# VectorE instructions on neighbouring 512-wide blocks merged, and PSUM tiles of two banks, in a two-layer encoder

## The chip, the core and the metric

The kernel runs on one core of a Trainium2 chip. TensorE (PE in the profile; PEld are its weight loads) multiplies into PSUM, VectorE (DVE) and ScalarE (ACT) work element by element, GpSimd (POOL) does small jobs, SyncE (SP) issues most of the DMAs. PSUM has eight banks, each one 128x512 fp32 result wide. The metric is the device time of one execution in microseconds (us); less is better.

## What is computed

A trunk of two layers over 256 tokens of width 2048, batch 1, in fp32:

```python
for l in range(DEPTH):
    h = rms_norm(x, g_mix[l])
    z = h @ (w_in_a[ia] if l % 2 == 0 else w_in_b[ib])
    tok_out = chunked_spatial_gating(...) if l % 2 == 0 else gqa_axial_attention(...)
    mem_out = memory_attention(q_mem, mem, g_mem[l], w_mem_kv[l], g_mq[l], g_mk[l])
    x = x + jnp.concatenate([tok_out, mem_out], axis=-1) @ w_out[l]
    x = x + swiglu(rms_norm(x, g_ffn[l]), w_gate_up[l], w_down[l])

def swiglu(h, w_gate_up, w_down):
    gate, up = jnp.split(h @ w_gate_up, 2, axis=-1)
    return (jax.nn.silu(gate) * up) @ w_down
```

The FFN is 5632 wide. Every weight is read once.

## The kernel before

**Precision.** Each operand of a product is split into a high part (a cast to fp32r, ScalarE, L192 and L254) and a low part (operand minus high part, VectorE, L193 and L255). `matmul3` (L196) then makes three matmuls: high by high, low by high, high by low. Weights are the moving operand, 512 columns wide; activations, transposed in 128x128 pieces on TensorE (L204), are the stationary one.

**Weights.** A weight tile `raw` holds four 128x512 blocks and comes by DMAs on SyncE's queue; four such tiles exist. `halves` (L248) makes its `whi` and `wlo` tiles, of which there are three each. In the mixers, `Linear.run` (L271) calls it with a step of two blocks, so that a unit of four blocks takes two casts and two subtractions; then come 24 matmuls, two blocks by two token tiles at a time. `Linear` has one accumulator bank for each of the two token tiles, out of the four of the pool `psa`.

**The FFN.** A `Pair` (L310) computes two neighbouring 512-column results for both token tiles: four results, from weight blocks w00, w10 (first column block, two rows of blocks) and w01, w11 (second). Its units are of two kinds. `eight` (L381) is the plain one: eight block products into banks 2 and 3 (token tile 0) and 4 and 8 (token tile 1). `seven` (L367) is a fast scheme with seven block products, on sums of weights and sums of activations: products 1, 5, 6 and 7 go to "inner" banks out of the pool `psm`, products 2, 3 and 4 into the outer banks. `prepare` (L339) fetches a unit's weights and, for a fast one, makes the four weight sums with four 512-wide additions (L347 to L350): t1 and t2, t3, t4 in `raw[:, 0]` and the tile `T`. It runs one unit ahead. After a Pair's last fast unit `inner` (L393) combines the four inner banks into e, f, v, y with one ScalarE copy and four VectorE instructions; for the down projection they are added into the residual x some steps later (L405). When the Pair's last unit is done `outer` (L408) adds banks 2 and 3, then 4 and 8, to the results (L413), one bank at a time.

A gate/up Pair's results go through SiLU (L785, L786) and are transposed some steps later by `turn_a` (L764), which takes a `misc` tile (L81), splits it and lets it go. `misc` tiles are single banks from `psm`, which has four; the mixers' transposes, attention scores and so on use them too. The FFN's eleven Pairs run in chunks of 4, 4 and 3, and after each chunk two Pairs of the down projection add into x.

**Order.** `later` and `tick` (L96, L99) place side work so many steps (half units) behind the point where it is queued. The program order that results is then reordered per engine by a planner that simulates the program and lets ready instructions go ahead of waiting ones; on the chip each engine runs its list in order. Tile pools are rings: a tile waits until the readers of the one before it in its place are done.

Of the kernel before, what the change touches and what calls it, by code (L numbers as in the profile page):

```python
# [10 lines left out]
F32 = mybir.dt.float32  # L11
# [5 lines left out]
P = 128  # L17
# [10 lines left out]
NB = 512  # L28
# [25 lines left out]
def encoder(ctx: ExitStack, tc: tile.TileContext, x, mem, g_mix, g_ffn, w_in_a, g_v_a, w_spatial, b_spatial,  # L54
# [10 lines left out]
    psa = ctx.enter_context(tc.tile_pool(name="psa", bufs=4, space=PS))  # L65
    psm = ctx.enter_context(tc.tile_pool(name="psm", bufs=4, space=PS))
# [13 lines left out]

    def misc():  # L81
        return psm.tile([P, NB], F32, tag="m", name=nm("m"))
# [37 lines left out]
    X = [[xp.tile([P, NB], F32, name=f"x_{t}_{j}") for j in range(4)] for t in range(NT)]  # L120
# [10 lines left out]
    def gain_columns(kind):  # L131
        gcol[kind] = const.tile([P, 32], F32, name=f"gcol_{kind}")
        gps = misc()
        nc.tensor.transpose(gps[:, :32], gst[kind], ident[:32, :32])
        nc.vector.tensor_copy(gcol[kind], gps[:, :32])
# [112 lines left out]
    def halves(raw, n, step=KC4):  # L248
# [3 lines left out]
        for c in range(0, n, step):  # L252
            cut = slice(c, min(c + step, n))
            nc.scalar.copy(hi[:, cut], raw[:, cut])  # L254
            nc.vector.tensor_tensor(lo[:, cut], raw[:, cut], hi[:, cut].bitcast(F32), ALU.subtract)  # L255
        return [(hi[:, c, :], lo[:, c, :]) for c in range(n)]

    class Linear:


        def __init__(self, parts, w, n0, nk=KD):
            self.parts, self.w, self.n0, self.left, self.first, self.raw = parts, w, n0, nk, True, {}
            self.acc = [psa.tile([P, NB], F32, tag="acc", name=nm("acc")) for _ in range(NT)]
# [7 lines left out]
        def run(self, units):  # L271
            for k0, n in units:
# [3 lines left out]
                parts = halves(raw[:, :n], n, KC2)  # L276
# [33 lines left out]
    class Pair:  # L310
# [5 lines left out]
        def __init__(self, parts, sums, w, na, nb, order, fast, into=None):  # L316
            self.parts, self.sums, self.w, self.na, self.nb, self.into = parts, sums, w, na, nb, into
            self.bank, self.part, self.ready = {}, {}, {}
# [20 lines left out]
        def prepare(self, i):  # L339
# [5 lines left out]
            if i in self.fast:  # L345
                T = room["p"].tile([P, KC3, NB], F32, tag="T", name=nm("T"), bufs=2)
                nc.vector.tensor_tensor(raw[:, 0], raw[:, 0], raw[:, 1], ALU.add)  # L347
                nc.vector.tensor_tensor(T[:, 0], raw[:, 0], raw[:, 3], ALU.add)
                nc.vector.tensor_tensor(T[:, 1], T[:, 0], raw[:, 1], ALU.subtract)
                nc.vector.tensor_tensor(T[:, 2], T[:, 0], raw[:, 2], ALU.add)  # L350
# [9 lines left out]
        def add(self, name, a, b):  # L360
            if name not in self.bank:
                self.bank[name] = misc() if name in (1, 5, 6, 7) else psa.tile([P, NB], F32, tag="acc", name=nm("acc"))
                self.part[name] = 0
# [3 lines left out]
        def seven(self, i, raw, T):  # L367
            t1, w00, w10, w11 = halves(raw, KC4)
            t2, t3, t4 = halves(T, KC3)
            get, (q5, s2, q7, q3) = self.parts.get, self.sums[i]  # L370
            k0, k1 = 2 * i, 2 * i + 1
            inner = [(1, get(k0, 0), w00), (5, q5, t1), (6, s2, t2), (7, q7, t3)]
            outer = [(2, get(k1, 0), w10), (3, q3, w11), (4, get(k1, 1), t4)]
            if self.bank:
                inner, outer = inner[:1] + outer[:2], inner[1:] + outer[2:]
# [17 lines left out]
        def inner(self):  # L393

            b, o = self.bank, self.into
            e, v, f, y = [room["p"].tile([P, NB], F32, tag=f"e{i}", name=nm("e"), bufs=1) for i in range(4)]
            nc.scalar.copy(e, b[1])
            nc.vector.tensor_tensor(v, b[6], e, ALU.subtract)
            nc.vector.tensor_tensor(f, b[5], v, ALU.add)
            nc.vector.tensor_tensor(v, b[7], v, ALU.add)  # L400
            nc.vector.tensor_tensor(y, b[7], f, ALU.add)
            if o:
                for (t, n), x, op in (((0, 0), e, ALU.add), ((0, 1), f, ALU.add), ((1, 0), v, ALU.subtract),
                                      ((1, 1), y, ALU.add)):
                    later(1 + 2 * t + n, lambda o=o[t][n], x=x, op=op: nc.vector.tensor_tensor(o, o, x, op))  # L405
            self.out = o or [[e, f], [v, y]]

        def outer(self, t):  # L408

            o = self.out  # L410
            for n, name in enumerate(((2, 3), (4, 8))[t]):
                op = ALU.subtract if name == 4 and not self.into else ALU.add
# [435 lines left out]
```

## Time and profile before

| | |
|---|---|
| runs before | median 2039.67 us of 3, 2039.08 to 2039.71 |
| profiled execution | span 2038.5 us, from first to last instruction (the page gives no other time of it) |
| HBM read | 390.26 MB, 194 GB/s over the span |
| weight casts L254 (ScalarE), on `raw` | 465 instructions, 700.8 us |
| weight subtractions L255 (VectorE), on `raw` | 465 instructions, 836.4 us |
| matmuls | 9298, most of them 128x512 |

A row of the groups reads: line, engine, operation, written tile <- read tiles, shape, count | busy us in all, mean ns of one | us that the engine sat idle just before them, and what ended most of that. A row of the timeline reads: start us, length us, engine, line, operation; in square brackets the engine's idle time ahead of it. A row of the stretches gives the stretch's borders and length, then each engine's busy us and instruction count, the clock granted to TensorE, the share of DMA time and GB/s.

### The profile page before, as it was taken

The numbers are of one execution on the slowest core, as the hardware profiler recorded it, in microseconds if no ns is written. First come the engines' busy times: TensorE is split into PE (matmuls) and PEld (weight loads), VectorE is DVE, ScalarE is ACT, GpSimd is POOL, SyncE is SP. The second block draws the span as 40 slices with busy tenths as digits, with TensorE's granted clock in tenths as the row PEclk, the third lists the DMA queues.
The fourth block names the chain that finished last, engine by engine and source line by source line (L and its number), as shares of the span: only waits on it lengthen the run. The fifth ranks groups of instructions, "written<-read, shape, count | busy, mean of one in ns | idle before, by whom it ended". The sixth has DMA issues, their size and how long they took to land.

```text
span 2038.5 us, 24693 instructions
## 1 busy us (share of the span) xinstructions
PE 2027.7 (99%) x9298; PEld 1679.9 (82%) x9298; DVE 1605.0 (79%) x1862; ACT 1095.0 (54%) x1389; POOL 50.6 (2%) x80
## 2 busy tenths in 40 slices
PE   9999999999999999999999999999999999999999
PEld 7888888888888888888888888888888888888887
DVE  5675557998879988887566886589979899798876
ACT  7765455454445554444555765555544455444552
POOL 2010000000000000000010100000000000000000
PEclk9999999999999999999999999999999999999999
DMA  9754554646656465665566544555566555565554
GB/s 325 253 179 155 185 188 154 227 165 206 203 190 227 165 207 196 202 227 194 186 198 204 173 133 141 202 185 178 195 206 218 195 184 190 205 221 192 183 197 137
DMA packets 202432, 396.08 MB, mean 194 GB/s; under 512 B 11068, under 2 KB 11432, under 8 KB 202312
## 3 DMA queue, kind: packets, MB, share of 16 engines
q1 hardware_dynamic: 198800, 385.79, 56.6%
q0 software_dynamic: 2048, 6.42, 1.0%
q10 hardware_dynamic: 1464, 2.28, 0.3%
q8 instruction: 73, 1.20, 0.2%
q14 instruction: 47, 0.39, 0.1%
HBM read 390.26 MB, written 4.19 MB: 194 GB/s over the span
## 4 chain that ended last, share of the span: by engine, by line
PE 96%; DVE 3%; DMA 1%; issue 1%; ACT 0%; SPq 0%; DVEq 0%; ACTq 0%
PE acc L200 27%; PE acc L199 27%; PE acc L198 27%; PE m L200 4%; PE m L198 4%; PE m L199 4%; PE m L204 2%; DVE wlo L255 1%; DMA raw<-in_w_gate_up 1%; PE m L500 0%; PE m L643 0%; ACT whi L254 0%; DVE x L413 0%; DVE e L413 0%; DMA x<-in_x 0%
## 5 line engine op out<-in xcount | busy, mean ns | idle before, releaser
L254 ACT CAST whi<-raw 128x2048 fp32r<-128x2048 f32 (+2 forms) x465 | 700.8, 1539 | 585.0 <-PE acc L199 512.5
L255 DVE TENSOR_TENSOR wlo<-raw,whi 128x2048 fp32r<-128x2048 f32 (+2 forms) x465 | 836.4, 1823 | 223.9 <-ACT whi L254 220.1
L198 PE MATMUL acc<-whi,h 128*128 128x512 f32 x1440 | 563.7, 392 | 0.0
L199 PE MATMUL acc<-whi,h 128*128 128x512 f32 x1440 | 562.6, 391 | 0.0
L200 PE MATMUL acc<-wlo,h 128*128 128x512 f32 x1440 | 524.1, 392 | 0.9 <-DVE wlo L255 0.9
L198 PE MATMUL acc<-whi,a 128*128 128x512 f32 x1062 | 414.8, 391 | 0.0
L199 PE MATMUL acc<-whi,a 128*128 128x512 f32 x1062 | 414.2, 390 | 0.0
L200 PE MATMUL acc<-wlo,a 128*128 128x512 f32 x1062 | 398.2, 391 | 0.0
L200 PEld LDWEIGHTS acc<-wlo,h 128*128 128x128 f32 x1440 | 270.6, 188 | 56.6 <-DVE wlo L255 1.5
L199 PEld LDWEIGHTS acc<-whi,h 128*128 128x128 f32 x1440 | 270.7, 188 | 55.3
L198 PEld LDWEIGHTS acc<-whi,h 128*128 128x128 f32 x1440 | 271.0, 188 | 54.0
L200 PEld LDWEIGHTS acc<-wlo,a 128*128 128x128 f32 x1062 | 199.4, 188 | 41.3 <-DVE wlo L255 0.3
L199 PEld LDWEIGHTS acc<-whi,a 128*128 128x128 f32 x1062 | 199.5, 188 | 40.4
L198 PEld LDWEIGHTS acc<-whi,a 128*128 128x128 f32 x1062 | 199.5, 188 | 40.2
L254 ACT CAST whi<-T 128x1536 fp32r<-128x1536 f32 x82 | 121.4, 1480 | 143.8 <-PE acc L199 102.2
L255 DVE TENSOR_TENSOR wlo<-T,whi 128x1536 fp32r<-128x1536 f32 x82 | 143.5, 1750 | 39.1 <-ACT whi L254 39.0
L198 PE MATMUL m<-whi,a 128*128 128x512 f32 x264 | 104.2, 395 | 0.7 <-ACT whi L254 0.7
L199 PE MATMUL m<-whi,a 128*128 128x512 f32 x264 | 102.9, 390 | 0.0
L347 DVE TENSOR_TENSOR raw<-raw 128x512 f32<-128x512 f32 x82 | 56.1, 684 | 54.9 <-DMA raw<-in_w_gate_up 53.5
L200 PE MATMUL m<-wlo,a 128*128 128x512 f32 x264 | 89.6, 389 | 0.0
L192 ACT CAST a<-m 128x512 fp32r<-128x512 f32 x80 | 46.7, 587 | 42.8 <-PE m L204 31.7
L193 DVE TENSOR_TENSOR a<-m,a 128x512 fp32r<-128x512 f32 x80 | 53.8, 682 | 13.1 <-ACT a L192 12.9
(126 smaller groups left out, 1473.1 us busy)
## 6 DMA issues: line engine op xcount, KB each, us to landing
raw<-in_w_gate_up SPq DMA_DIRECT2D x352, 512.0 KB, 4.7
raw<-in_w_down SPq DMA_DIRECT2D x176, 512.0 KB, 5.2
raw<-in_w_out SPq DMA_DIRECT2D x32, 1024.0 KB, 5.1
raw<-in_w_in_a SPq DMA_DIRECT2D x24, 1024.0 KB, 5.2
raw<-in_w_in_b SPq DMA_DIRECT2D x24, 1024.0 KB, 5.1
raw<-in_w_mem_kv SPq DMA_DIRECT2D x16, 1024.0 KB, 5.1
raw<-in_w_in_a SPq DMA_DIRECT2D x7, 512.0 KB, 6.2
x<-in_x SPq DMA_DIRECT2D x8, 256.0 KB, 5.8
```

What stands on the lines that cost most here:

```text
L192: nc.scalar.copy(hi, src)
L193: nc.vector.tensor_tensor(lo, src, hi.bitcast(F32), ALU.subtract)
L198: nc.tensor.matmul(out, lhsT=a[0], rhs=b[0], start=start, stop=False)
L199: nc.tensor.matmul(out, lhsT=a[1], rhs=b[0], start=False, stop=False)
L200: nc.tensor.matmul(out, lhsT=a[0], rhs=b[1], start=False, stop=stop)
L204: nc.tensor.transpose(dst[:, c * P:(c + 1) * P], src[:, c * P:(c + 1) * P], ident)
L254: nc.scalar.copy(hi[:, cut], raw[:, cut])
L255: nc.vector.tensor_tensor(lo[:, cut], raw[:, cut], hi[:, cut].bitcast(F32), ALU.subtract)
L347: nc.vector.tensor_tensor(raw[:, 0], raw[:, 0], raw[:, 1], ALU.add)
```

## The change

Six things change.
- `Linear.run` calls `halves` on whole units: one cast and one subtraction over up to four blocks.
- `prepare` makes the weight sums with three additions, the first over two blocks with a broadcast operand: t1 and t3 in `T[:, :2]`, then t2 in `raw[:, 0]`, then t4 in `T[:, 2]`. `seven` takes t1 and t2 from the places where they now lie, and its inner products come in the order 1, 6, 5, 7; product 6 joins the first group where banks are open already.
- `inner` keeps its results in one tile `E` of four blocks: one copy, one subtraction, one addition over banks 5 and 7, one scalar-tensor-tensor form; the last block has the opposite sign to y. The sums into x go two blocks at a time.
- `outer` adds two banks with one instruction.
- PSUM tiles: `psa` has two tiles of two banks; a Linear's accumulators, or a Pair's banks (2,3) and (4,8), are the halves of one. The pool of inner banks and `misc` tiles is opened anew in each stage: four single banks in a mixer, two tiles of two banks in an FFN. There (1,6) and (5,7) are a tile each, and a `misc` tile takes a whole two-bank tile and uses half of it.
- x and the results are tiles of two neighbouring blocks.

```diff
-    psa = ctx.enter_context(tc.tile_pool(name="psa", bufs=4, space=PS))
-    psm = ctx.enter_context(tc.tile_pool(name="psm", bufs=4, space=PS))
+    psa = ctx.enter_context(tc.tile_pool(name="psa", bufs=2, space=PS))
...
+    def open_rooms(scope, name, tiles, banks):
+
+        room["p"] = scope.enter_context(tc.tile_pool(name=name, bufs=tiles, reuse_waits="tile"))
+        room["m"] = scope.enter_context(tc.tile_pool(name=f"ps_{name}", bufs=4 // banks, space=PS))
+        room["banks"] = banks
+
+    def banks2(pool, tag):
+        return pool.tile([P, 2, NB], F32, tag=tag, name=nm(tag))
+
     def misc():
-        return psm.tile([P, NB], F32, tag="m", name=nm("m"))
+        if room["banks"] == 2:
+            return banks2(room["m"], "m")[:, 0]
+        return room["m"].tile([P, NB], F32, tag="m", name=nm("m"))
...
-    X = [[xp.tile([P, NB], F32, name=f"x_{t}_{j}") for j in range(4)] for t in range(NT)]
+    X2 = [[xp.tile([P, 2, NB], F32, name=f"x_{t}_{i}") for i in range(2)] for t in range(NT)]
+    X = [[X2[t][j // 2][:, j % 2] for j in range(4)] for t in range(NT)]
...
-    def halves(raw, n, step=KC4):
+    def halves(raw, n):
 
         hi = wp.tile([P, KC4, NB], F32R, tag="whi", name=nm("whi"))[:, :n]
         lo = wp.tile([P, KC4, NB], F32R, tag="wlo", name=nm("wlo"))[:, :n]
-        for c in range(0, n, step):
-            cut = slice(c, min(c + step, n))
-            nc.scalar.copy(hi[:, cut], raw[:, cut])
-            nc.vector.tensor_tensor(lo[:, cut], raw[:, cut], hi[:, cut].bitcast(F32), ALU.subtract)
+        nc.scalar.copy(hi, raw)
+        nc.vector.tensor_tensor(lo, raw, hi.bitcast(F32), ALU.subtract)
         return [(hi[:, c, :], lo[:, c, :]) for c in range(n)]
...
-            self.acc = [psa.tile([P, NB], F32, tag="acc", name=nm("acc")) for _ in range(NT)]
+            acc = banks2(psa, "acc")
+            self.acc = [acc[:, t] for t in range(NT)]
...
-                parts = halves(raw[:, :n], n, KC2)
+                parts = halves(raw[:, :n], n)
...
-                nc.vector.tensor_tensor(raw[:, 0], raw[:, 0], raw[:, 1], ALU.add)
-                nc.vector.tensor_tensor(T[:, 0], raw[:, 0], raw[:, 3], ALU.add)
-                nc.vector.tensor_tensor(T[:, 1], T[:, 0], raw[:, 1], ALU.subtract)
-                nc.vector.tensor_tensor(T[:, 2], T[:, 0], raw[:, 2], ALU.add)
+                w01 = raw[:, 0].unsqueeze(1).to_broadcast([P, 2, NB])
+                nc.vector.tensor_tensor(T[:, :2], raw[:, 1:4:2], w01, ALU.add)
+                nc.vector.tensor_tensor(raw[:, 0], T[:, 0], raw[:, 3], ALU.add)
+                nc.vector.tensor_tensor(T[:, 2], raw[:, 0], raw[:, 2], ALU.add)
...
-                self.bank[name] = misc() if name in (1, 5, 6, 7) else psa.tile([P, NB], F32, tag="acc", name=nm("acc"))
-                self.part[name] = 0
+                both = next(b for b in ((1, 6), (5, 7), (2, 3), (4, 8)) if name in b)
+                inner = name in (1, 5, 6, 7)
+                self.tile[both] = banks2(room["m"] if inner else psa, "m" if inner else "acc")
+                for i, one in enumerate(both):
+                    self.bank[one], self.part[one] = self.tile[both][:, i], 0
...
-            t1, w00, w10, w11 = halves(raw, KC4)
-            t2, t3, t4 = halves(T, KC3)
+            t2, w00, w10, w11 = halves(raw, KC4)
+            t1, t3, t4 = halves(T, KC3)
...
-            inner = [(1, get(k0, 0), w00), (5, q5, t1), (6, s2, t2), (7, q7, t3)]
+            inner = [(1, get(k0, 0), w00), (6, s2, t2), (5, q5, t1), (7, q7, t3)]
             outer = [(2, get(k1, 0), w10), (3, q3, w11), (4, get(k1, 1), t4)]
             if self.bank:
-                inner, outer = inner[:1] + outer[:2], inner[1:] + outer[2:]
+                inner, outer = inner[:1] + outer[:2] + inner[1:2], inner[2:] + outer[2:]
...
-            b, o = self.bank, self.into
-            e, v, f, y = [room["p"].tile([P, NB], F32, tag=f"e{i}", name=nm("e"), bufs=1) for i in range(4)]
-            nc.scalar.copy(e, b[1])
-            nc.vector.tensor_tensor(v, b[6], e, ALU.subtract)
-            nc.vector.tensor_tensor(f, b[5], v, ALU.add)
-            nc.vector.tensor_tensor(v, b[7], v, ALU.add)
-            nc.vector.tensor_tensor(y, b[7], f, ALU.add)
...
+            b = self.bank
+            E = room["p"].tile([P, 4, NB], F32, tag="e", name=nm("e"), bufs=1)
+            v = E[:, 3]
+            nc.scalar.copy(E[:, 0], b[1])
+            nc.vector.tensor_tensor(v, b[6], E[:, 0], ALU.subtract)
+            nc.vector.tensor_tensor(E[:, 1:3], self.tile[5, 7], v.unsqueeze(1).to_broadcast([P, 2, NB]), ALU.add)
+            nc.vector.scalar_tensor_tensor(E[:, 3], b[5], -1.0, E[:, 2], ALU.mult, ALU.subtract)
+            if self.into:
+                for t, op in enumerate((ALU.add, ALU.subtract)):
+                    later(1 + 2 * t, lambda t=t, op=op: nc.vector.tensor_tensor(self.into[t], self.into[t],
+                                                                                E[:, 2 * t:2 * t + 2], op))
+            self.out = self.into or [E[:, :2], E[:, 2:]]
...
-            o = self.out
-            for n, name in enumerate(((2, 3), (4, 8))[t]):
-                op = ALU.subtract if name == 4 and not self.into else ALU.add
-                nc.vector.tensor_tensor(o[t][n], self.bank[name], o[t][n], op)
+            op = ALU.subtract if t and not self.into else ALU.add
+            nc.vector.tensor_tensor(self.out[t], self.tile[((2, 3), (4, 8))[t]], self.out[t], op)
...
-        room["p"] = scope.enter_context(tc.tile_pool(name=f"mix{l}", bufs=MIX_TILES, reuse_waits="tile"))
+        open_rooms(scope, f"mix{l}", MIX_TILES, 1)
...
-        room["p"] = scope.enter_context(tc.tile_pool(name=f"ffn{l}", bufs=FFN_TILES, reuse_waits="tile"))
+        open_rooms(scope, f"ffn{l}", FFN_TILES, 2)
```

More of the change, by code (lines that the diff above doesn't have):

```diff
@@ L132, in gain_columns @@
         gcol[kind] = const.tile([P, 32], F32, name=f"gcol_{kind}")
-        gps = misc()
+        gps = misc() if room else banks2(psa, "acc")[:, 0]
         nc.tensor.transpose(gps[:, :32], gst[kind], ident[:32, :32])
@@ L317, in __init__ @@
             self.parts, self.sums, self.w, self.na, self.nb, self.into = parts, sums, w, na, nb, into
-            self.bank, self.part, self.ready = {}, {}, {}
+            self.bank, self.tile, self.part, self.ready = {}, {}, {}, {}
             self.order, self.fast = order, fast
@@ L393, in inner @@
         def inner(self):
-            b, o = self.bank, self.into
-            e, v, f, y = [room["p"].tile([P, NB], F32, tag=f"e{i}", name=nm("e"), bufs=1) for i in range(4)]
-            nc.scalar.copy(e, b[1])
-            nc.vector.tensor_tensor(v, b[6], e, ALU.subtract)
-            nc.vector.tensor_tensor(f, b[5], v, ALU.add)
[L400 to L406, printed above, removed]
+            b = self.bank
[10 more added lines that the diff above has]
+            self.out = self.into or [E[:, :2], E[:, 2:]]
         def outer(self, t):
-            o = self.out
-            for n, name in enumerate(((2, 3), (4, 8))[t]):
-                op = ALU.subtract if name == 4 and not self.into else ALU.add
-                nc.vector.tensor_tensor(o[t][n], self.bank[name], o[t][n], op)
+            op = ALU.subtract if t and not self.into else ALU.add
+            nc.vector.tensor_tensor(self.out[t], self.tile[((2, 3), (4, 8))[t]], self.out[t], op)
     def head_norm(acc, r, gain, rope=False):
@@ L736, in encoder @@
             add_residual(linear(cat, w_out[l], j * NB, units), j, norm, gslice("ffn", l), hF)
-        room.pop("p")
+        room.clear()
         scope.close()
         scope = ExitStack()
-        room["p"] = scope.enter_context(tc.tile_pool(name=f"ffn{l}", bufs=FFN_TILES, reuse_waits="tile"))
+        open_rooms(scope, f"ffn{l}", FFN_TILES, 2)
         sums = {}
@@ L784, in encoder @@
                     a = kp.tile([P, NB], F32, tag="sg", name=nm("sg"), bufs=2)
-                    nc.scalar.activation(a, g.out[t][0], AF.Silu, scale=norm.r[t])
-                    nc.vector.scalar_tensor_tensor(a, g.out[t][1], norm.r[t], a, ALU.mult, ALU.mult)
+                    nc.scalar.activation(a, g.out[t][:, 0], AF.Silu, scale=norm.r[t])
+                    nc.vector.scalar_tensor_tensor(a, g.out[t][:, 1], norm.r[t], a, ALU.mult, ALU.mult)
                     later(3 + t if f == chunk[-1] else 12 + t, lambda a=a, t=t, f=f: turn_a(a, t, f))
@@ L795, in encoder @@
                     order.insert(2 * n + (0 if jj and not last else 2), i)
-                into = [[X[t][2 * jj + n] for n in range(2)] for t in range(NT)]
+                into = [X2[t][jj] for t in range(NT)]
                 pairs.append(Pair(aT, aS, w_down[l], 2 * jj * NB, (2 * jj + 1) * NB, order, quick, into))
@@ L811, in encoder @@
         norm = next_norm
-        room.pop("p")
+        room.clear()
         scope.close()
```

## The prediction, made before the change was run

> **What bounds the kernel now.** I read the page from the top, engines first, then the slices of the span and the chain that ended last.
>
> ```profile
> span 2038.5 us, 24693 instructions
> ...
> PE 2027.7 (99%) x9298; PEld 1679.9 (82%) x9298; DVE 1605.0 (79%) x1862; ACT 1095.0 (54%) x1389; POOL 50.6 (2%) x80
> ...
> PE   9999999999999999999999999999999999999999
> ...
> PEclk9999999999999999999999999999999999999999
> ...
> PE 96%; DVE 3%; DMA 1%; issue 1%; ACT 0%; SPq 0%; DVEq 0%; ACTq 0%
> ```
>
> TensorE is busy in every slice at full granted clock, and 96% of the chain is matmuls. The change adds and removes no matmul, so it can win only what TensorE waits. The view of busy time by stretch, cut where the chain leaves TensorE, shows how little that is.
>
> ```profile
> core 0: us, PE busy (x) PEld busy (x) DVE busy (x) ACT busy (x) POOL busy (x), PEclk, DMA share, GB/s
> 0.00:50.00 50.00, 45.30 (x201) 35.98 (x202) 29.02 (x55) 37.27 (x95) 11.64 (x27) 1.00 0.93 323
> 350.00:376.00 26.00, 24.84 (x107) 19.59 (x106) 25.96 (x29) 15.93 (x13) 0.00 (x0) 1.00 0.49 165
> 376.00:780.00 404.00, 404.00 (x1812) 333.64 (x1811) 347.90 (x333) 207.89 (x154) 0.00 (x0) 1.00 0.59 198
> 780.00:802.00 22.00, 21.82 (x97) 17.59 (x96) 22.00 (x25) 8.61 (x5) 0.00 (x0) 1.00 0.57 192
> 1345.00:1385.00 40.00, 39.70 (x174) 32.13 (x173) 36.12 (x47) 22.55 (x20) 0.00 (x0) 1.00 0.48 163
> 1790.00:1812.00 22.00, 21.83 (x96) 17.58 (x95) 21.04 (x21) 7.80 (x5) 0.00 (x0) 1.00 0.58 190
> 2030.00:2038.50 8.50, 4.19 (x19) 3.14 (x17) 2.77 (x4) 0.00 (x0) 0.00 (x0) 1.00 0.34 123
> ```
>
> From 376 to 780 us the FFN runs undisturbed, 1812 matmuls in 404 us, 0.223 us each. At that rate the 107 matmuls of 350 to 376 need 23.9 us, so 2.1 are lost; 97 need 21.6 of 22 (0.4 lost), 174 need 38.8 of 40 (1.2), 96 need 21.4 of 22 (0.6). Together 4.3 us, and there VectorE is busy nearly throughout. These four stretches are all that less VectorE work can win. The 4.7 idle us of the first 50 wait for the first loads and for casts of one or two blocks, whose form the change leaves alone. Last come 8.5 us with the output.
>
> **The change part by part.** Durations by form:
>
> ```profile
> L255 DVE TENSOR_TENSOR wlo<-raw,whi 128x2048 fp32r<-128x2048 f32 x264 | 599.5, 2285 | 105.5 <-ACT whi L254 104.5
> L254 ACT CAST whi<-raw 128x2048 fp32r<-128x2048 f32 x264 | 499.9, 1914 | 482.4 <-PE acc L199 427.9 <-issue 39.0 <-DVE T L348 4.4
> L255 DVE TENSOR_TENSOR wlo<-raw,whi 128x1024 fp32r<-128x1024 f32 x199 | 235.5, 1220 | 116.5 <-ACT whi L254 113.7 <-PE acc L200 1.7 <-PE m L204 0.7
> L254 ACT CAST whi<-raw 128x1024 fp32r<-128x1024 f32 x199 | 199.7, 1050 | 102.4 <-PE acc L199 84.5 <-issue 11.4 <-DMA raw<-in_w_in_a 4.9
> L347 DVE TENSOR_TENSOR raw<-raw 128x512 f32<-128x512 f32 x82 | 56.1, 684 | 54.9 <-DMA raw<-in_w_gate_up 53.5 <-DMA raw<-in_w_down 1.4
> L413 DVE TENSOR_TENSOR e<-acc,e 128x512 f32<-128x512 f32 x88 | 58.2, 682 | 3.7 <-PE acc L200 3.1
> L786 DVE SCALAR_TENSOR_TENSOR sg<-e,s,sg 128x512 f32<-128x512 f32 x44 | 32.5, 742 | 0.0
> ```
>
> By duration two 512-wide additions cost 1.37 us and one 1024-wide 1.22. But queued instructions overlap, as VectorE's timeline shows (start, length, and what sat idle before):
>
> ```profile
> 788.14 0.68 DVE L400 TENSOR_TENSOR e<-m,e 128x512 f32<-128x512 f32 x1
> 788.74 0.68 DVE L401 TENSOR_TENSOR e<-m,e 128x512 f32<-128x512 f32 x1
> ...
> 797.02 4.47 DVE L255 TENSOR_TENSOR wlo<-raw,whi 128x2048 fp32r<-128x2048 f32 x2
> ...
> 40.80 2.36 DVE L255 TENSOR_TENSOR wlo<-raw,whi 128x1024 fp32r<-128x1024 f32 x2 [2.97 <-ACT whi L254]
> ```
>
> A 512 form holds the engine 0.60 us (788.74 - 788.14), a 1024 form 1.14 (2.36 - 1.22), a 2048 form 2.19 (4.47 - 2.28). One merge saves 0.06 us, in the mixers' weight halves 0.09.
> - Weight sums (82 times): 4 x 0.60 becomes 1.14 + 2 x 0.60, 4.9 us of VectorE in all.
> - Inner results (32): one merge, given back by the scalar form (742 against 682 ns). Nothing.
> - Sums into x: 40 become 20, 1.2 us. Block results: 136 become 68, 4.1 us.
> - Mixer halves: of the 199 pairs of 1024 form, 7 belong to two-block units of the first linear; 192 become 96, 96 x 0.09 = 8.6 us, and 96 casts go on ScalarE.
>
> That is 19 us of 1605, and where TensorE is never idle it is worth nothing: matmuls cover it. In each of the four stretches lie some five merges (two or three weight sums, two block results), so 5 x 0.06 = 0.3 us may return in each: -1.2. Bounds: 0 and -4.3.
>
> Here a page speaks. The Trainium skill, "VectorE: DVE Perf Modes", section on the TRN2 errata, says that the fixed latency is paid between instructions and gives (N+151)/0.96 ns for an fp32 tensor_tensor; an estimate by that page is 2 x 691 - 1224 = 158 ns per merge, or 0.8 us in a stretch, with which the sum below would be lower by about 1.4. The 0.60 us spacing decides against it for queued instructions, so I keep 0.06.
>
> What coarser pieces delay:
>
> ```profile
> 47.24 2.36 DVE L255 TENSOR_TENSOR wlo<-raw,whi 128x1024 fp32r<-128x1024 f32 x2 [4.09 <-ACT whi L254]
> ...
> 52.24 0.39 PE L200 MATMUL acc<-wlo,h 128*128 128x512 f32 x1
> ```
>
> Mixer halves: a unit's first two blocks are ready later by (1.91 - 1.05) + (2.29 - 1.22) = 1.9 us. The tightest four-block unit is the one whose load came late: its first half ends at 48.46 and, counting subtractions against matmuls in order, is first read at 52.24. The cover is 3.8 us, 1.9 stay. Cost 0; without that cover each linear's late unit would cost up to 1.9.
>
> Weight sums: `raw[:, 0]`, which the cast of the whole tile waits for, is now final after 1.14 + 0.60 = 1.74 us, not after one 0.68. In the FFN, sums are prepared a unit ahead (24 matmuls, 5.4 us), which hides 1.1. Where the load itself was late, on the chain of waits,
>
> ```profile
> 1353.32 4.54 DMA raw<-in_w_gate_up
> 1357.95 0.69 DVE raw L347
> ```
>
> the cast may start 1.1 us later. Bounds 0 and +1.1; I take +0.4, as the remaining sums stood ahead of its subtraction before too.
>
> PSUM: the accumulators rotate as before, two linears or one Pair. New is that in the FFN each transpose tile takes a two-bank tile, of two, which `inner` groups (1,6) and (5,7) need as well. The tightest place is the start of a down projection, where the last block's transposes come just ahead of the first fast unit:
>
> ```profile
> 502.62 0.60 PE L204 MATMUL m<-ident,sg 128*128 128x128 f32 x4
> ...
> 505.81 0.60 PE L204 MATMUL m<-ident,sg 128*128 128x128 f32 x4
> ...
> 505.82 0.68 DVE L193 TENSOR_TENSOR a<-m,a 128x512 fp32r<-128x512 f32 x1
> ...
> 506.16 0.48 PE L198 MATMUL m<-whi,a 128*128 128x512 f32 x1
> ...
> 507.76 2.29 DVE L255 TENSOR_TENSOR wlo<-raw,whi 128x2048 fp32r<-128x2048 f32 x1 [1.26 <-ACT whi L254]
> ...
> 509.97 0.68 DVE L193 TENSOR_TENSOR a<-m,a 128x512 fp32r<-128x512 f32 x1
> ...
> 515.12 0.39 PE L198 MATMUL m<-whi,a 128*128 128x512 f32 x1
> ```
>
> The first tile is free at 506.50, the second at 510.65; the unit's matmuls start at 506.16. Groups 1, 6, 2, 3 and 4 (15 matmuls, 3.4 us) do not need the second tile and reach 509.6; the next unit's weights are complete at 510.05. So TensorE has work but for about half a microsecond, and high-part matmuls fill that. Behind a waiting matmul stand all later ones, in order. Bounds 0 and 510.65 - 506.16 = 4.5 us in each of five places (two chunks of layer 0, three of layer 1): 0 to +22. I take 0.
>
> The tail:
>
> ```profile
> 2032.87 0.69 DVE L413 TENSOR_TENSOR x<-acc,x 128x512 f32<-128x512 f32 x1 [0.67 <-PE acc L200]
> ...
> 2033.80 0.39 PE L200 MATMUL acc<-wlo,a 128*128 128x512 f32 x1
> ...
> 2034.23 0.69 DVE L413 TENSOR_TENSOR x<-acc,x 128x512 f32<-128x512 f32 x1 [0.67 <-PE acc L200]
> 2034.95 0.36 ACTq L809 DMA_DIRECT2D out<-x  x1
> ```
>
> Now block 4 is added at 2032.87, while block 8's matmuls run; merged, both start at 2034.23 and take 1.22: +0.53. Then SyncE issues column 2's store ahead of column 3's (+0.36, as the issue on ScalarE), and both land together: another 256 KB, up to 0.8 us at the 323 GB/s of the first stretch. Bounds +0.5 and +1.7; I take +1.0. The Trainium skill's "Perfetto Trace Analysis", section Optimizing Scalar/DVE Operations, says that grouping helps a saturated engine and that breaking up helps where an unsaturated one holds up others. The idle 0.67 us ahead of the last addition agrees.
>
> **Sum:** -1.2 + 0.4 + 0 + 1.0 = +0.2 us on the span of 2038.5. The median of the runs, 2039.67, lies 1.17 us above it; carried over, 2038.7 + 1.17 = 2039.9.
>
> **The rivals.** (1) Slower: the shared two-bank tiles bind at the down projections. For it: the second tile is held 4.8 us, and ScalarE and VectorE work in order, so one more 2.29 us subtraction ahead of it lengthens that. Against it: the matmuls' order already goes around such waits, for the same unit's last inner group starts at 515.12, behind the next unit's. It decides where the tile is held beyond 3.4 us and the next unit's parts are not there; then at least 510.65 - 509.56 = 1.1 us is lost in each of five places: 2039.9 + 5.5 = 2045.4. "Perfetto Trace Analysis", section Matmuls, of the Trainium skill asks that independent groups rotate through different banks; this change has fewer tiles to rotate through. (2) Faster: VectorE was late by a hair in the four stretches, and a shorter queue frees all 4.3 us: 2039.67 - 4.3 + 1.0 = 2036.4. For it: VectorE 25.96 of 26 us. Against: five merges give 0.3. (3) The merged forms, with a stride or a broadcast operand that no row shows, run like two: nothing is saved, 2039.67 + 0.4 + 1.0 = 2041.1.
>
> **How the numbers follow.** Forecast (2038 to 2042.5) 0.62, rival 1 0.16, rival 2 0.12, rival 3 0.10. The measurement tells about 0.2% apart, 4.1 us: under 2035.6 or over 2043.7. Under it only the edge of rival 2, 0.04; over it rival 1 and 0.02 of the rest, 0.18; within 0.78. The range takes in rivals 2 and 1 to a little past their values: 2036.4 to 2046.
>
> **What would show it.** Right: 1564 VectorE and 1293 ScalarE instructions, TensorE still 0.223 us per matmul between 376 and 780, the four stretches shorter by tenths, the last addition 1.22 us. Wrong: matmuls that wait for a transpose tile's subtraction, or any matmul in the mixers that waits beyond 1 us; a median outside the range; or a spacing of matmuls other than 0.223, which nothing here prices.

## The result and the profile after

The changed kernel took 2086.36 us, median of four runs (2083.80 to 2088.74), against 2039.68 before on the same chip: a ratio of 1.0228, 95% interval 1.0214 to 1.0243. It is 2.3% slower, 46.7 us, and far outside the forecast range.

The page of the changed kernel: span, busy time of each engine, the chain that ended last by engine.

```profile
span 2082.0 us, 24239 instructions
...
PE 2038.0 (98%) x9298; PEld 1678.8 (81%) x9298; DVE 1585.9 (76%) x1564; ACT 1087.2 (52%) x1293; POOL 57.2 (3%) x80
...
PE 87%; ACT 5%; DVE 5%; DMA 2%; issue 1%; SPq 0%; ACTq 0%; DVEq 0%
```

VectorE is busy 19.1 us less than before, as worked out, and the span is 43.5 us longer. The matmuls are as many, but TensorE's share of the chain fell from 96% to 87%, and most of that went to ScalarE and VectorE: TensorE waits where it did not.

The view of waits of the kernel before, TensorE's alone (who waits, for whom, us in all, times, longest):

```profile
PE m L134 <- DMA gst_mix<-in_g_mix: 4.3, 1, 4.3
PE acc L200 <- DVE wlo L255: 0.9, 1, 0.9
```

Two more rows, of 0.7 and 0.3 us, end it.

The first six rows of the same view of the changed kernel (in its code the three matmuls are L209 to L211, the cast L263, the subtraction L264, the weight sums L358 to L360, the block result L424, the gating GELU L706):

```profile
PE acc L209 <- ACT a L706: 11.5, 2, 10.5
PE m L209 <- ACT whi L263: 8.3, 21, 1.8
PE m L215 <- DMA x<-in_x: 5.0, 2, 4.7
PE acc L209 <- DVE e L424: 4.6, 4, 1.1
PE acc L211 <- DVE wlo L264: 3.8, 6, 1.1
PE acc L209 <- DVE a L442: 3.5, 2, 1.9
```

New are one wait of 10.5 us for a GELU in the first mixer, 21 short ones for casts (four of 0.2 us at most before), four of about 1.1 us for merged block results and two for the mixers' head norm (L442); the waits for low halves rose from 0.9 to 3.8 us. TensorE's last matmul starts at 2076.28 us, against 2033.80 before: 42.5 of the 43.5 us are lost on the way there, the rest behind it. The matmuls themselves are no slower where nothing waits; by stretch, changed kernel:

```profile
650.00:680.00 30.00, 30.00 (x136) 24.84 (x135) 23.91 (x18) 15.62 (x11) 0.00 (x0) 1.00 0.68 229
```

and before:

```profile
650.00:680.00 30.00, 30.00 (x136) 24.85 (x135) 29.79 (x33) 16.54 (x14) 0.00 (x0) 1.00 0.60 205
```

Both do 136 matmuls in those 30 us.

**The long wait.** The chain of waits of the changed kernel from 106 us on:

```profile
106.13 0.39 ACT a L237
106.53 1.88 ACT whi L263
108.43 2.29 DVE wlo L264
110.73 0.27 DVE a L238
...
117.20 0.46 ACT a L706
117.78 0.70 ACT a L706
118.52 0.79 PE acc L209
119.31 0.43 PE acc L210
```

TensorE began to wait at 107.7. The GELU that frees its accumulators stands on ScalarE behind a cast of 1.88 us and behind the memory's pieces (L237), which alternate one by one with VectorE (L238) and so wait for the subtraction of 2.29 us. Before, ScalarE ran this GELU at 104.5, ahead of that cast:

```profile
104.46 0.69 ACT L695 ACTIVATE a<-acc,s 128x512 f32<-128x512 f32 x1
...
105.61 2.00 ACT L254 CAST whi<-raw 128x1024 fp32r<-128x1024 f32 x2
```

In the changed kernel, after the wait, seven matmuls take 0.43 us and more instead of 0.23. The granted clock (the number behind the engines' busy times) tells why:

```profile
107.70:118.50 10.80, 0.31 (x3) 0.07 (x1) 4.66 (x8) 6.84 (x18) 0.00 (x0) 0.67 0.59 207
118.50:121.60 3.10, 3.08 (x7) 2.48 (x8) 1.65 (x5) 3.01 (x14) 0.75 (x2) 0.50 0.14 48
121.60:125.00 3.40, 3.40 (x16) 2.75 (x15) 2.85 (x8) 3.24 (x15) 1.70 (x4) 0.99 0.00 0
```

The seven take 3.1 us; at 0.227 us each they would take 1.6, so half rate costs another 1.6 us or so. The Trainium skill, "TensorE: Matmul & The Clock Gate", section Part 1: The HAM clock gate, says that the clock halves after an idle window of about 3.4 us and comes back after about as long a busy one; these rows agree, with 10.8 us idle and some 3 us at half rate. Other runs show half rate behind shorter waits as well; the last section has them.

### The profile page after: what moved, and what is told of

The parts are those of the page before. It is cut to its first block, busy times and chain, and to the rows that moved or that the text cites. A ratio compares the mean times of both kernels' runs of the same rounds, so it can differ in the third digit from the quotient of the medians.

```text
span 2082.0 us, 24239 instructions
## 1 busy us (share of the span) xinstructions
PE 2038.0 (98%) x9298; PEld 1678.8 (81%) x9298; DVE 1585.9 (76%) x1564; ACT 1087.2 (52%) x1293; POOL 57.2 (3%) x80
## 4 chain that ended last, share of the span: by engine, by line
PE 87%; ACT 5%; DVE 5%; DMA 2%; issue 1%; SPq 0%; ACTq 0%; DVEq 0%
PE acc L211 25%; PE acc L209 24%; PE acc L210 24%; PE m L209 4%; ACT whi L263 4%; PE m L210 4%; PE m L211 4%; DVE wlo L264 3%; PE m L215 2%; DMA raw<-in_w_in_a 1%; DMA raw<-in_w_down 0%; DMA raw<-in_w_gate_up 0%; DVE T L358 0%; ACT sg L796 0%; PE m L511 0%
## 5 line engine op out<-in xcount | busy, mean ns | idle before, releaser
L264 DVE TENSOR_TENSOR wlo<-raw,whi 128x2048 fp32r<-128x2048 f32 (+2 forms) x369 | 833.6, 2262 | 334.8 <-ACT whi L263 334.1
L263 ACT CAST whi<-raw 128x2048 fp32r<-128x2048 f32 (+2 forms) x369 | 696.2, 1890 | 650.6 <-PE acc L210 532.9
L209 PE MATMUL acc<-whi,h 128*128 128x512 f32 x1440 | 564.5, 392 | 3.4 <-DVE a L442 1.9
L211 PE MATMUL acc<-wlo,h 128*128 128x512 f32 x1440 | 549.2, 391 | 1.3 <-DVE wlo L264 1.3
L209 PE MATMUL acc<-whi,a 128*128 128x512 f32 x1062 | 416.9, 393 | 17.0 <-ACT a L706 10.5
L211 PE MATMUL acc<-wlo,a 128*128 128x512 f32 x1062 | 410.0, 391 | 2.5 <-DVE wlo L264 2.5
L209 PEld LDWEIGHTS acc<-whi,h 128*128 128x128 f32 x1440 | 270.6, 188 | 60.1 <-DVE a L442 2.1
L211 PEld LDWEIGHTS acc<-wlo,h 128*128 128x128 f32 x1440 | 270.2, 188 | 58.2 <-DVE wlo L264 2.6
L209 PEld LDWEIGHTS acc<-whi,a 128*128 128x128 f32 x1062 | 199.9, 188 | 60.8 <-ACT a L706 10.8
L211 PEld LDWEIGHTS acc<-wlo,a 128*128 128x128 f32 x1062 | 199.7, 188 | 45.4 <-DVE wlo L264 4.2
L263 ACT CAST whi<-T 128x1536 fp32r<-128x1536 f32 x82 | 121.5, 1482 | 166.0 <-PE acc L210 166.0
L264 DVE TENSOR_TENSOR wlo<-T,whi 128x1536 fp32r<-128x1536 f32 x82 | 144.0, 1756 | 58.3 <-ACT whi L263 38.7
L358 DVE TENSOR_TENSOR T<-raw 128x1024 f32<-128x1024 f32 x82 | 100.2, 1222 | 8.8 <-DMA raw<-in_w_gate_up 4.4
L209 PE MATMUL m<-whi,a 128*128 128x512 f32 x264 | 103.3, 391 | 2.7 <-ACT whi L263 2.7
L211 PE MATMUL m<-wlo,a 128*128 128x512 f32 x264 | 98.8, 390 | 0.2 <-DVE wlo L264 0.2
L209 PEld LDWEIGHTS m<-whi,a 128*128 128x128 f32 x264 | 49.6, 188 | 14.9 <-ACT whi L263 4.8
```

Of the source, the lines that this page charges most:

```text
L209: nc.tensor.matmul(out, lhsT=a[0], rhs=b[0], start=start, stop=False)
L211: nc.tensor.matmul(out, lhsT=a[0], rhs=b[1], start=False, stop=stop)
L263: nc.scalar.copy(hi, raw)
L264: nc.vector.tensor_tensor(lo, raw, hi.bitcast(F32), ALU.subtract)
L358: nc.vector.tensor_tensor(T[:, :2], raw[:, 1:4:2], w01, ALU.add)
```

## The experiments

Two theories at first: the mixers' merged halves (one long cast and subtraction per unit), or the PSUM tiles of two banks with the merged block results. Each part was undone by itself, and two were done alone on the kernel before. All ratios are to the kernel before on the same chip (2039.9 to 2041.0 us), with 95% intervals.

**u_halves**: the changed kernel, mixers' halves in two steps.

```diff
-                parts = halves(raw[:, :n], n)
+                parts = halves(raw[:, :n], n, KC2)
```

> The changed kernel with the mixers' weight halves made in two steps again. Theory 'order' (the merged casts move the GELU behind one more weight cast in ScalarE's program, and TensorE waits 10.5 us for it, then runs 14 matmuls at 0.43 us instead of 0.23): these 10.5 + 2.9 us come back, about 2073 us, and the rest of the waits stays. Theory 'banks' (an accumulator tile of two banks is let go only when both halves are read): the wait for the GELU stays, about 2086 us.

2075.37 us, 1.0175 (1.0160 to 1.0190). For the GELU this is theory 'order': its wait fell to 0.3 us. The 21 waits for casts stayed (8.1 us), and one of 4.9 us for a head norm came up at 1188 us.

**b_halves**: the kernel before with the merged halves alone.

```diff
-                parts = halves(raw[:, :n], n, KC2)
+                parts = halves(raw[:, :n], n)
```

> The kernel before with the mixers' weight halves merged, nothing else. Theory 'order': a wait for the GELU of about 10 us appears near 108 us, 2050 to 2053 us. Theory 'banks': without two-bank accumulators nothing waits, 2039 to 2041 us.

2060.03 us, 1.0098 (1.0082 to 1.0115): 20 us from an edit that was costed at nothing. Its waits:

```profile
PE acc L198 <- ACT a L695: 9.2, 1, 9.2
...
PE m L500 <- DVE a L490: 4.0, 1, 4.0
```

The first is the GELU again. The other is in the second mixer; the chain of waits there:

```profile
1186.29 1.91 ACT whi L254
1188.23 2.29 DVE wlo L255
1190.60 0.59 DVE s L481
1191.18 0.53 DVE a L490 x2
1191.71 1.04 DVE a L431 x4
1192.79 0.80 PE acc L198
```

A softmax's scaling (L490, 0.35 us an instruction), for which TensorE's transposes wait, stands on VectorE behind the 2.29 us subtraction, which itself waits for the cast. Both waits are followed by matmuls at half rate. Added up start to start: 9.3 and 4.2 us of waiting, 2.2 and 3.4 of slow matmuls, together 19.1 of the 19.4 us by which its span is longer (2057.9 against 2038.5).

**u_acc**: the changed kernel with four single accumulator banks again, the block results one bank at a time.

```diff
-            acc = banks2(psa, "acc")
-            self.acc = [acc[:, t] for t in range(NT)]
+            self.acc = [psa.tile([P, NB], F32, tag="acc", name=nm("acc")) for _ in range(NT)]
...
-            nc.vector.tensor_tensor(self.out[t], self.tile[((2, 3), (4, 8))[t]], self.out[t], op)
+            for n, name in enumerate(((2, 3), (4, 8))[t]):
+                nc.vector.tensor_tensor(self.out[t][:, n], self.bank[name], self.out[t][:, n], op)
```

> The changed kernel with four single accumulator banks, and block results added one bank at a time. Theory 'banks': the waits for the GELU (11.5 us, with 2.9 at half rate), for the block results (4.6) and for the head norm (3.5) go, about 2064 us. Theory 'order': only the last two go, about 2078 us, and a wait of some 10 us for the GELU stays near 108 us.

2060.94 us, 1.0104 (1.0089 to 1.0120). Neither theory had it: the 21 waits for casts, which both took to stay, became one of 1.8 us. Those for block results went, the GELU's stayed (9.2 us), as theory 'order' said, and b_halves' 4.0 us at the softmax came up.

**u_acc_halves**: the diffs of u_halves and u_acc together.

> The changed kernel with two parts undone at once: the accumulators are four single-bank tiles again (block results added bank by bank), and the mixers' weight halves are cast in two steps. What stays: merged weight sums, merged inner results, two-bank inner tiles of the FFN. Theory 'these two parts are the whole loss, and they add up': u_acc took 25.4 us off the changed kernel and u_halves 11.0, so both should give 2040 to 2051 us, no GELU wait over 1 us, and few waits of m<-whi. Rival 'the parts that stay cost something too': 2055 us or more.

2042.14 us, 1.0007 (0.9997 to 1.0016). The two parts are nearly the whole loss, 44.2 of 46.7 us. They do not simply add up: undone singly they gave 25.4 and 11.0 us, 36.4 together, since with one undone new waits come up for the other (the softmax's 4.0 us in u_acc, the head norm's 4.9 in u_halves). What is left, merged weight sums, merged inner results and two-bank inner tiles, costs 2 us at most by the medians, and the interval includes none.

**u_sums**: the changed kernel with the four weight sums of before; **u_sums_order** also puts the products back in the order that goes with them (the last two edits below are its alone).

```diff
-                w01 = raw[:, 0].unsqueeze(1).to_broadcast([P, 2, NB])
-                nc.vector.tensor_tensor(T[:, :2], raw[:, 1:4:2], w01, ALU.add)
-                nc.vector.tensor_tensor(raw[:, 0], T[:, 0], raw[:, 3], ALU.add)
-                nc.vector.tensor_tensor(T[:, 2], raw[:, 0], raw[:, 2], ALU.add)
+                nc.vector.tensor_tensor(raw[:, 0], raw[:, 0], raw[:, 1], ALU.add)
+                nc.vector.tensor_tensor(T[:, 0], raw[:, 0], raw[:, 3], ALU.add)
+                nc.vector.tensor_tensor(T[:, 1], T[:, 0], raw[:, 1], ALU.subtract)
+                nc.vector.tensor_tensor(T[:, 2], T[:, 0], raw[:, 2], ALU.add)
...
-            inner = [(1, get(k0, 0), w00), (6, s2, t2), (5, q5, t1), (7, q7, t3)]
+            inner = [(1, get(k0, 0), w00), (5, q5, t1), (6, s2, t2), (7, q7, t3)]
...
-                inner, outer = inner[:1] + outer[:2] + inner[1:2], inner[2:] + outer[2:]
+                inner, outer = inner[:1] + outer[:2], inner[1:] + outer[2:]
```

> The changed kernel with the four 512-wide weight sums of before. Theory: the cast of a fast unit's weights is late because the first block of the tile is final only after 1.74 us; the 21 waits of 0.4 us for casts ahead of the inner products (8.3 us) go, about 2078 us. Rival: those waits come from the inner and transpose tiles' two banks; they stay, about 2086 us.

> The changed kernel with the four weight sums of before and, unlike u_sums, also the order of the products that goes with them (product 5 from the raw tile first, product 6 later). Theory 'u_sums was slower than the changed kernel only because it left product 6 in front while its weight came out of the later cast': at or a little below the changed kernel, 2080 to 2088 us, and the waits for wlo fall back to about 4 us. Rival 'the merged sums gain about 10 us in the changed kernel': 2094 us or more.

2096.94 us, 1.0286 (1.0266 to 1.0306), and 2098.35, 1.0282 (1.0268 to 1.0296). Both are slower than the changed kernel: there the merged sums gain 11 to 12 us. The waits for casts stayed in u_sums (8.2 us), so the late first block does not cause them, and the order of the products is not why it is slow. In u_sums_order TensorE waits 9.5 us for low halves, more than twice as much as in the changed kernel:

```profile
PE m L211 <- DVE wlo L264: 5.2, 8, 2.6
...
PE acc L211 <- DVE wlo L264: 4.3, 6, 1.9
```

Waits of the outer products for casts rose as well, from 0.5 to 4.0 us, and two waits of 1.8 us are followed by half rate here, some 1.5 us each. A likely reading is that one instruction more ahead of the subtraction counts where TensorE waits for VectorE already; no run shows that by itself.

**b_sums**: the kernel before with the merged sums and their order of products.

> The kernel before with the merged weight sums alone (and the order of the products that goes with them). The prediction put them at +0.4 us with bounds of 0 to +1.1, 2039.7 to 2040.8 us here. Rival 'they move the order of casts as the halves do': 2044 us or more. Rival 'they gain': below 2038 us.

2042.38 us, 1.0011 (1.0002 to 1.0019). Without those waits the merge gains nothing and costs some 2 us, the interval reaching from 0.4 to 3.9: none of the three ranges has the median, and the prediction's bounds lie partly in the interval.

**Why the halves cost 20 us. b_halves_order** puts one cast of b_halves behind the GELU, where the kernel before has it (as a constraint on ScalarE's order alone).

```diff
-            nc.scalar.copy(hi[:, cut], raw[:, cut])
+            with tc.issue_after(gelu[0].ins) if uid[0] == 211 else ExitStack():
+                nc.scalar.copy(hi[:, cut], raw[:, cut])
```

> b_halves (the kernel before with the mixers' weight halves in one step, 2060.03 us), with one cast, the one of weight tile whi_210, put behind the third gating block's GELU on ScalarE, where the kernel before has it. No instruction is added or taken away. Theory 'what the merge costs there is the order on ScalarE': the GELU wait of 9.2 us and the half-rate matmuls after it (14 x 0.2 us) go, 2046 to 2050 us. Rival 'the longer cast and subtraction cost it, wherever they stand': the wait comes back at a neighbouring unit, 2057 us or more.

2057.04 us, 1.0081 (1.0066 to 1.0096): by the time just inside the rival's range, by the waits neither. The wait fell from 9.2 to 5.3 us, not to nothing, and the only other one at this line is 0.8 us. The GELU now ran at 111.1 us (114.0 in b_halves, 104.5 before), still behind the memory's pieces. As many of them stand ahead of it as before (60), so it is not their order: the long steps had delayed them from several units earlier on. (The expectation's 14 slow matmuls were a miscount; there are some ten.)

**b_halves_local** keeps the merge except in the two stretches with the waits, 23 units of 96.

```diff
-                parts = halves(raw[:, :n], n)
+                parts = halves(raw[:, :n], n, KC2 if 100 < uid[0] < 215 or 1450 < uid[0] < 1620 else KC4)
```

> b_halves (2060.03 us) with the weight halves in two steps again in two stretches of the program alone: the gating blocks and the query product of the first mixer (about 40 to 110 us), and the products around the self-attention's scores in the second mixer (about 1130 to 1205 us). Everywhere else in the mixers they stay merged. Theory 'the merge costs only where a short step that TensorE waits for queues behind the long cast and subtraction, at 107 us and at 1187 us': both waits go, 2039 to 2043 us. Rival 'the long steps cost a little everywhere, and new waits come up elsewhere': 2048 us or more.

2042.40 us, 1.0009 (1.0000 to 1.0018). The other 73 units cost some 2 us together (the interval reaches 3.7). The merge is expensive in two places, where a short step that TensorE waits for queues behind the long ones.

**Why the accumulators cost 33 us** (2075.37 - 2042.14). **u_halves_outer** is u_halves with the block results added bank by bank (the diff of `outer` above) on the same two-bank tiles.

> u_halves (2075.37 us) with the block results added bank by bank again, while the accumulators stay two-bank tiles. Theory 'it is the tile of two banks, which is released as a whole and of which there are only two': the 21 short waits of m<-whi (8.1 us) stay, the four at the starts of the down projections shrink at most in part, 2068 to 2076 us. Rival 'it is the merged addition, which comes later': the waits go, 2058 us or less.

2076.20 us, 1.0171 (1.0156 to 1.0187), as u_halves: the waits for casts stay (9.0 us, 17 of them), and so do those for block results (4.8 us, against 3.5). The merged addition by itself is not the cause; the tile is.

**u_halves_stage** is u_halves with single banks in the mixers and two-bank tiles in the FFN. For this the accumulators' pool is opened anew in each stage, which no run tries by itself.

> u_halves (2075.37 us) with four single-bank accumulators in the two mixers alone; the FFN keeps its tiles of two banks and its merged block results. Theory 'most of the accumulators' loss is the FFN's': the head-norm wait of 4.9 us and the half-rate matmuls behind it go, the 21 waits of m<-whi and the four at the down projections stay: 2063 to 2070 us. Rival 'the mixers' accumulators are most of it': 2055 us or less.

2063.05 us, 1.0110 (1.0095 to 1.0125). So the mixers' accumulators cost 12.3 us and the FFN's 20.9. In the mixers the head norm's wait of 4.9 us and some 2.3 us lost at half rate behind it are gone; the other 5 are not traced to a place. The chain of waits of u_halves there:

```profile
1187.74 1.03 DVE a L444 x4
1188.78 2.27 DVE wlo L266 x2
...
1192.32 1.05 DVE a L444 x4
...
1193.41 0.80 PE acc L209
```

The head norm (L444) reads the accumulator of the first token tile, then that of the second, with two subtractions and other steps in between. TensorE starts behind the second reading: the tile that holds both comes free no earlier.

The 21 waits are the FFN's. One of them, TensorE's timeline of u_halves_stage (start, length, engine, line, operation, shape, idle time before; L211 and L212 multiply high halves, L213 low ones):

```profile
453.76 0.39 PE L211 MATMUL acc<-whi,h 128*128 128x512 f32 x1
...
455.12 0.39 PE L212 MATMUL acc<-whi,h 128*128 128x512 f32 x1
455.75 0.50 PE L211 MATMUL m<-whi,h 128*128 128x512 f32 x1 [0.23 <-ACT whi L267]
...
456.32 0.40 PE L213 MATMUL acc<-wlo,h 128*128 128x512 f32 x1
```

and the same place in u_acc_halves, with single banks (its lines are L209 to L211):

```profile
454.84 0.39 PE L209 MATMUL acc<-whi,h 128*128 128x512 f32 x1
...
456.43 0.39 PE L210 MATMUL acc<-whi,h 128*128 128x512 f32 x1
456.65 0.39 PE L209 MATMUL m<-whi,h 128*128 128x512 f32 x1
...
457.11 0.39 PE L211 MATMUL acc<-wlo,h 128*128 128x512 f32 x1
```

In both, the last product shown is the first that needs the current unit's low half, and the `m` products in front of it belong to the next unit and need its cast. With four single tiles, eight products of the high half go ahead of them (two for each of the accumulators 609, 610, 611 and 616); with two tiles of two banks it is four. The lists of instructions, cut to the run in question:

```
two-bank tiles: acc_603<-whi_607 x2, acc_604<-whi_599 x2, acc_604<-wlo_600, acc_604<-whi_607 x2,
                m_601<-whi_610 x2, acc_603<-wlo_608
single banks:   acc_609<-whi_614 x2, acc_610<-whi_614 x2, acc_611<-whi_614 x2, acc_616<-whi_614 x2,
                m_607<-whi_618 x2, acc_609<-wlo_615
```

In these lists all writes to one tile stand in program order. The reading: a low-half product that the planner takes to be not ready blocks the rest of its tile, and with two chains instead of four the planner runs out of high-half products sooner and takes up the next unit's, whose cast on the chip is some 0.4 us away. Two runs test this from two sides.

**u_stage_hifirst**: u_halves_stage with the FFN's products written in another order, in each group first those with high weight halves, then those with low ones.

```diff
-                for name, a, b in some:
-                    self.add(name, a, b)
+                for low in [self.add(name, a, b) for name, a, b in some]:
+                    low()
...
+            return lambda: nc.tensor.matmul(self.bank[name], lhsT=a[0], rhs=b[1], start=False, stop=last)
```

> u_halves_stage (2063.05 us: accumulators of two banks and merged block results in the FFN alone) with the FFN's products traced in another order: of each group, first all products with the high halves of the weights, then those with the low halves. Tiles, merged additions and the number of instructions stay. Theory 'products into one tile run in program order, so with two tiles in place of four TensorE has half as many products to do before it needs the low half or the next cast': the 21 waits for whi and the four for wlo go for the most part, 2042 to 2052 us. Rival 'the tile is released as a whole, and the additions come late': the waits stay, 2058 us or more.

2050.78 us, 1.0049 (1.0034 to 1.0064): 12.3 us back with tiles and merged additions kept. In its waits those for casts in the FFN are gone, and those for low halves too; what is left besides the start and 1.0 us outside the FFN is

```profile
PE acc L381 <- DVE e L433: 7.9, 5, 2.2
...
PE acc L381 <- DVE x L433: 1.8, 1, 1.8
```

**u_stage_order**: u_halves_stage with the next unit's first inner product pinned on TensorE behind all products written before it.

```diff
-        nc.tensor.matmul(out, lhsT=a[0], rhs=b[0], start=start, stop=False)
+        first = nc.tensor.matmul(out, lhsT=a[0], rhs=b[0], start=start, stop=False)
+        if room.get("keep"):
+            tc.keep_in_program_order(first)
...
+            room["keep"] = name == 1
```

> u_halves_stage (2063.05 us) with the first inner product of each unit pinned on TensorE behind all products written before it. Theory 'the order inside a tile': the waits for whi become waits for wlo, since the products ahead of it need the low half: 2058 to 2066 us. Rival 'the planner only puts that inner product too early': the 6.8 us of whi waits go and nothing takes their place, 2050 to 2056 us.

2053.45 us, 1.0060 (1.0045 to 1.0075). Here the rival was right: the waits for casts go, and none for low halves take their place (3.1 us, as in u_halves_stage); those for block results rise from 4.9 to 7.1 us. So the current unit's low half is there in time on the chip; the planner only did not count on it. Both runs say that the 21 waits are a matter of the order that the two tiles bring with them, not of the banks.

The rest is the other rival, release as a whole. The chain of waits of u_stage_hifirst at the start of a down projection:

```profile
486.92 5.08 DMA raw<-in_w_down
...
492.09 1.23 DVE T L361
493.31 1.15 DVE e L433
...
494.60 0.47 PE acc L381
```

The next Pair's outer tile is the one that the last Pair's merged addition (L433) must empty. That addition stands on VectorE behind a weight sum which waits for its load, and TensorE waits for it, 2.6 us from one matmul's start to the next's. In u_acc_halves, where each accumulator is a tile of its own and is added by itself, the same stretch has no such wait. These waits are 9.7 us in u_stage_hifirst and 4.8 in the changed kernel. No run splits the additions with this order of products; with the other order u_halves_outer did, and the waits stayed.

**u_hifirst**: the whole change with that order of products.

> The whole change (2086.36 us) with that order of products in the FFN and nothing else. Theory: what the FFN's accumulators cost comes back, some 15 to 21 us; the mixers' halves (11 to 20 us with the GELU wait of 10.5 us) and the mixers' accumulators stay: 2062 to 2072 us. Rival (release as a whole): 2080 us or more.

2075.98 us, 1.0176 (1.0159 to 1.0193). It lies between the two ranges. 10.4 us come back, not 15 to 21: the waits for casts are gone (no such row), but the head norm's rose from 3.5 to 7.2 us and the block results' from 4.8 to 10.1, and two of these waits are followed by half rate. The mechanism held, its size in the whole change was overrated.

**u_acc_halves_inner**: u_acc_halves with single inner banks in the FFN as well, and with them single banks for its transposes.

```diff
-                self.tile[both] = banks2(room["m"], "m")
+                self.bank[name] = misc() if name in (1, 5, 6, 7) else psa.tile([P, NB], F32, tag="acc", name=nm("acc"))
...
-            nc.vector.tensor_tensor(E[:, 1:3], self.tile[5, 7], v.unsqueeze(1).to_broadcast([P, 2, NB]), ALU.add)
+            nc.vector.tensor_tensor(E[:, 1], b[5], v, ALU.add)
+            nc.vector.tensor_tensor(E[:, 2], b[7], v, ALU.add)
```

> u_acc_halves (2042.14 us) with the inner products of the FFN on single banks too, and their two additions apart. Theory 'the tile of two banks costs the last 2 us as well': the wait of 1.8 us of m<-whi near the end goes, 2039.5 to 2041 us, the time of the kernel before. Rival 'the merged sums cost them': 2042 us or more, and b_sums the same.

2040.87 us, 1.0002 (0.9993 to 1.0012), against 1.0007 (0.9997 to 1.0016) for u_acc_halves: the wait of 1.8 us near the end went, but the medians are too close to call the inner tiles' price more than about 1 us. None of the runs beat the kernel before.

## Why the prediction was wrong

- **The floor** held: TensorE bounds the kernel, and no run with fewer VectorE instructions came out below the kernel before. VectorE came out 19.1 us less busy, as the text had it, with 1564 instructions, and the next instruction starts 1.13 us behind a merged one, where 1.14 was taken from the casts' subtractions, in the changed kernel's timeline:

```profile
424.57 1.23 DVE L358 TENSOR_TENSOR T<-raw 128x1024 f32<-128x1024 f32 x1
425.70 1.23 DVE L424 TENSOR_TENSOR e<-acc,e 128x1024 f32<-128x1024 f32 x1
```

  Rival 3 (merged forms run like two) fell with it. That saving was worth nothing, as said.
- **"Mixer halves: ... The cover is 3.8 us, 1.9 stay. Cost 0"** failed, by 20 us alone (b_halves) and 11 within the change. The step measured the cover for the matmuls that read these halves, and it held: 73 of 96 units cost some 2 us together. It did not ask the second question, which short instructions stand behind the longer ones on ScalarE and VectorE and who waits for them: the GELU that empties two accumulators, and the softmax's scaling. It also took the order of the two engines as given, though a planner sets it anew; that one cast ahead of the GELU was 3.9 of the 9.2 us wait, and 3.0 us of the time.
- **"PSUM: the accumulators rotate as before, two linears or one Pair"** failed, by 33 us with the halves in two steps. They hold as many results, but a tile is also the grain in which the program is ordered and released: two chains of writes instead of four put the next unit's product too early (21 waits, 12.3 of the FFN's 20.9 us by u_stage_hifirst), both banks must be added up before the next Pair may start in them (the other 8.6, by difference), and in the mixers the head norm holds both accumulators (7 of 12.3 us, with the slow matmuls; the rest stays open).
- **The two-bank inner tiles, "Bounds 0 and ... +22. I take 0"**: right, about 1 us, and no matmul waits for a transpose tile's subtraction. Rival 1, which was slower too, looked for the loss at the down projections and in the wrong pool: a wait is there, but for the accumulators.
- **Weight sums, +0.4 (0 to +1.1)**: +2.0 us in b_sums (0.4 to 3.9, so too low by the median, but not clearly), and of the other sign in the changed kernel, where they gain 11 to 12.
- **The tail, +1.0**: right. From the last matmul's start to the end of the span it is 2082.0 - 2076.28 = 5.7 us, against 2038.5 - 2033.80 = 4.7, and the last addition takes 1.23.
- **"Any matmul in the mixers that waits beyond 1 us"** was named as what would show it wrong, and does, at 107.7 us. The chances were wrong with it: 0.18 for slower came from one place alone, and the edits costed at zero carried no doubt of their own.
- The page that was cited for the tail, "Perfetto Trace Analysis" of the Trainium skill, section Optimizing Scalar/DVE Operations, was the one to apply to the halves: VectorE is at 76 to 79%, not saturated, and breaking up its 2.29 us subtraction, with ScalarE's 1.9 us cast, is what b_halves_local did in two stretches, for 17.6 us. Its other point, rotating through different banks (section Matmuls), names the right place; but u_stage_hifirst, with the same tiles, shows that 12.3 of the FFN's 20.9 us are the order of the products.

## What to carry to other kernels

Merging instructions on an engine that is not the bound can win nothing beyond the bound's own idle time, and it can lose where a short step that the bound engine waits for queues behind the longer one; look for those steps on each engine that the merge touches, not only for the readers of its result. Merging two PSUM results into one tile also merges their order of writes and their release: count the independent chains that TensorE has left, and write the products that are ready first in front. A planner that simulates may take any such edit as a reason to reorder work far away, so compare the lists of instructions around every urgent step, and give an edit of this kind a range to the slow side even if its own cost is zero.

## What the runs showed of the hardware

Some waits on TensorE cost more than their length. After the 10.8 us wait seven matmuls ran at a granted clock of 0.50, and after the 4.0 us wait of b_halves some eleven did, from 1192.8 to 1197.6 us:

```profile
1192.80:1196.00 3.20, 3.20 (x8) 2.52 (x9) 3.20 (x13) 0.72 (x3) 2.10 (x2) 0.50 0.69 268
```

After the 1.9 us wait that ends at 1173.9 us in the changed kernel the next stretch has the full clock,

```profile
1174.00:1178.00 4.00, 4.00 (x18) 3.31 (x19) 4.00 (x6) 3.94 (x17) 0.00 (x0) 1.00 0.19 22
```

but the length of one wait does not settle it. The 1.8 us wait for a cast near the end is followed by half rate in u_acc and by full clock in u_acc_halves:

```profile
2021.40:2024.80 3.40, 3.40 (x10) 2.65 (x10) 3.40 (x5) 0.00 (x0) 0.00 (x0) 0.51 0.81 211
```

```profile
2004.00:2008.00 4.00, 4.00 (x18) 3.23 (x18) 4.00 (x6) 0.00 (x0) 0.00 (x0) 1.00 0.82 224
```

Over all 17 traces, from 12 us on, 11 of the 27 waits of 1.7 to 2.9 us were followed by half rate, and so were all 13 of 4.0 us and more, but none shorter than 1.7. The first products of the kernel before lie 0.43 us apart as well (7.29 and 7.71 us), which the clock of 1.00 in the row of its first 50 us does not show. So a wait under 1.7 us brought no half rate, and a longer one may cost 1.4 to 3.4 us on top of its length; what decides between two waits of equal length is not shown here.
